# A two-layer attention trunk on one core: y loaded by 256 tokens, the last gate by token halves, score spans as steps of their own, and a running minimum

## The chip, the core and the metric

The kernel runs on one core of one Trainium2 chip. The metric is device time in microseconds of one execution; the kernel before has a median of 1973.18 us over 3 runs (1972.05 to 1976.23). The core has five engines that each work off their own queue in order: PE (TensorE; loads of weights are listed apart as PEld), DVE (VectorE), ACT (ScalarE), POOL (GpSimd) and SP (SyncE), which here issues every DMA.

## What is computed

The input x is 1024 tokens by 1024 channels in fp32. Two layers, each `h = h + rmsnorm(mixer(rmsnorm(h)))`; each mixer's input projection also gives a gate of the width of its output:

```python
for i in range(2):
    u = rmsnorm(h, norm_pre[i])
    y = dilated_mixer(u, ...) if i == 0 else diff_mixer(u, ...)
    h = h + rmsnorm(y, norm_post[i])
# diff_mixer, per head (8 heads, two parts c = 0, 1 of 64 channels, values of 128):
s = einsum(q, k) * scale                  # causal mask
p = softmax(s)
a = p[:, 0] - lam * p[:, 1]
o = rmsnorm(a @ v, subln) * (1 - lambda_init)
y = (o * silu(gate)) @ w_out
```

Layer 0 (dilated_mixer) has 16 heads in three groups of windows and dilations, whose outputs are weighed by their softmax denominators, then multiplied by silu(gate) and by the output weights in the same way.

## The kernel before

**Numbers and tiles.** PE multiplies fp32 values as a high and a low part, three matmuls for each product (hi by hi, hi by lo, lo by hi). `XH` and `XL` hold the two parts of the normalised input, transposed: 128 partitions, 8 blocks of channels (k-tiles), 1024 tokens. At the end of each layer the same two tiles are filled again with y, the gated output of the attention, for the product with the output weights.

**Stages of the span.** Up to about 400 us: values and gates of layer 0. To about 1210 us: the attention of layer 0 (scores L603, transposes L626, products L653 and L665). To about 1424 us: the output product of layer 0 (po L391), then values and most gates of layer 1. To about 1910 us: the attention of layer 1 (class DiffHead). The rest is the output product of layer 1.

**Filler.** In both attentions PE's order is written by hand: steps of the heads (a load, a block of scores, transposes, products, a norm, a gate) are sorted by a due time in units of heads, and after each step the class Filler issues matmuls of other work up to a goal that grows with the due time. That other work is, in this order: the projections of later heads' queries and keys (`qk_unit`, pqk L276; each is written to DRAM, `qk_d`, and read back by `heads_in`, L268 to L270), values, the last gates (`late_gates`, `gate_units`, pg L276), and `out_early` (L425), which forms the first half of the output product (pe L444) for 6 of the 8 token blocks from the first four k-tiles of y. Only PE's order is fixed by hand. The order of the other queues comes from a scheduler that builds on the program.

**The last gate and y.** y of the k-tiles 0 to 6 is written to DRAM (`put_y`, y_d L384) as its heads are done. The last gate is the last reader of the old XH and XL. It goes by k-tiles over both token halves, so that both PSUM banks of the tag `pj` are taken from its start: k-tiles 0 and 1 for half 0, then for half 1, then one k-tile at a time. `out_early` then loads y k-tile by k-tile (`load_y`, L402), each as two DMAs of 128 partitions x 1024 tokens, 512 KB, that follow the last reader of that k-tile. It yields until `stored` says that the k-tile's y is in DRAM. `part` (L449) is the copy of a block's partial output product out of PSUM; it is kept in XH and XL (L452), where the rows of the first k-tiles are free again, and read by the second part of the output product (`out_rest`, po L391).

**Heads of layer 1.** A DiffHead has two parts, s = 0 and 1. `load(part)` fetches queries (qh, ql) and keys (ka) of one part; both parts are due at h - 0.15, and the first also fetches the two value tiles vt, ahead of its queries and keys. The tiles qh, ql and ka have two buffers, so a head's two parts fill them and the next head's part can be loaded only when the last scores of the same part are done. `scores(i, s)` takes query block i: (i+1)*128 keys, in two spans of at most 512 columns from i = 4 on. Each span has two matmuls into a PSUM tile `sc` (tag `s`, 2 buffers), and a DVE instruction (L954, in the profile CUSTOM_DVE_ANT_0 with a read of its accumulator) that adds the mask, writes `pm` and gives the span's minimum. With two spans, L957 takes the smaller of both minima; for s = 0, L960 subtracts 10 ln 2 from it. ACT then takes the exponential (L961) with the sum as denominator `den`. For s = 1 DVE inverts it (L970), forms the factor k (L971) and combines both parts (L973). `transposes` (tp L984) splits the transposed result into ph (ACT, L989) and pl (DVE, L122), `product` multiplies by the values (ob L1004), `norm` and `gate` (L1045 to L1050) finish a half of 512 tokens and write y.

Of the kernel before, what the change touches and what calls it, by code (L numbers as in the profile page):

```python
# [10 lines left out]
F32 = mybir.dt.float32  # L11
# [20 lines left out]
SQ_LIMIT = 2.0 ** 64  # L32

# [3 lines left out]
SPAN, LAG, LAG_O, LAG_N, LAG_G, AHEAD = 0.85, 0.3, 0.2, 0.1, 0.15, 0.15  # L37
# [55 lines left out]
def trunk(ctx: ExitStack, tc: tile.TileContext, a: dict, out: bass.AP):  # L93
# [179 lines left out]
    def project(o, wh, wl, tok, kts=range(KT)):  # L273
        for kt in kts:
# [128 lines left out]

    def partial(n):
# [504 lines left out]
    with tc.tile_pool(name="l1", bufs=2) as lp:  # L909
        md = lp.tile([P, 640], F32, tag="md", name="md", bufs=1)  # L910
        nc.sync.dma_start(md, a["maskd"])
        class DiffHead:
# [7 lines left out]
            def load(self, part):  # L920
                fill.until(24 + self.h)
                fill.until(("v", self.h // 2))
                if part == 0:
                    self.den = lp.tile([P, NB], F32, tag="den", name="den")
                    self.fin = []
                    self.vt = []
# [6 lines left out]
                self.fin.append(heads_in(ep, 24 + self.h, part))  # L933

            def scores(self, i, s):
# [3 lines left out]
                if s == 0:  # L939
                    pm = lp.tile([P, wq], F32, tag=f"pm0{i}", name="pm0", bufs=1)  # L940
                else:
                    pm = lp.tile([P, T], F32, tag="pm1", name="pm1", bufs=1)
                mx = lp.tile([P, 4], F32, tag=f"mx{s}", name=f"mx{s}")
                den = self.den[:, i : i + 1] if s == 0 else mx[:, 3:4]
                cut = wq - max(256, wq - 512) if wq > 512 else 0
                spans = [(0, cut), (cut, wq)] if cut else [(0, wq)]
                for j, (k0, k1) in enumerate(spans):
                    w_ = k1 - k0
                    sc = ps.tile([P, 512], F32, tag="s", name="sc")
                    for k, q in enumerate((qh, ql)):  # L950
                        nc.tensor.matmul(  # L951
# [181 lines left out]
```

## Time and profile before

| | |
|---|---|
| median of 3 runs | 1973.18 us (1972.05 to 1976.23) |
| the profiled execution's own time | 1973.98 us |
| its span, first to last instruction | 1972.1 us |
| mean granted clock of PE | 0.986 |
| instructions | 29075 |
| ACT busy | 885.3 us (45%) |
| POOL busy | 784.2 us (40%) |
| bytes moved by DMA | 397.90 MB, 202 GB/s over the span |

The profile is of one execution. Its busy time by engine, the idle time ahead of an instruction with what ended it ("releaser"), tables of busy time by stretch of the span, and the granted clock of PE by stretch are read below. Times inside the span count from its start. 1973.98 - 1972.1 = 1.9 us of the execution lie outside the span.

### The profile page before, as it was taken

What the parts mean: (1) busy time and instruction counts of PE and PEld (TensorE: products, weight loads), DVE (VectorE), ACT (ScalarE), POOL (GpSimd) and SP (SyncE); (2) the same over time, 40 slices, a digit from 0 to 9 for tenths busy, and PEclk for the clock granted to TensorE, in tenths of its full rate; (3) what the DMA queues carried; (4) which work ended last, traced back from release to release, by engine and by line L of the source; (5) the groups of instructions that cost most, each with busy time, mean ns of one, the idle gap of its engine ahead of it and who ended that gap; (6) DMA issues with size and microseconds to landing.
All of it is one profiled execution on the core that took longest, in us unless ns stands there. A gap on an engine that the chain in (4) does not pass through costs nothing.

```text
span 1972.1 us, 29075 instructions
## 1 busy us (share of the span) xinstructions
PE 1888.0 (96%) x10008; PEld 1587.9 (81%) x10008; DVE 985.4 (50%) x2618; ACT 885.3 (45%) x2043; POOL 784.2 (40%) x553
## 2 busy tenths in 40 slices
PE   7999999999999999999999878999989899999897
PEld 5788888888888888888888767788878798897786
DVE  5311221135555555555555635550177877778626
ACT  4212112135656565656565555342244455446532
POOL 0000001154585867676776532320742435423011
PEclk9999999999999999999999979999999999999899
DMA  6424344277798989898989798442644565556643
GB/s 225 161 91 133 117 145 155 91 233 219 213 294 239 296 242 283 249 280 259 271 267 267 237 329 217 165 167 87 207 155 132 181 213 182 166 182 196 239 158 128
DMA packets 217539, 397.90 MB, mean 202 GB/s; under 512 B 40880, under 2 KB 123312, under 8 KB 217392
## 3 DMA queue, kind: packets, MB, share of 16 engines
q1 hardware_dynamic: 217392, 396.04, 63.8%
q8 instruction: 80, 1.31, 0.3%
q14 instruction: 67, 0.55, 0.1%
HBM read 254.87 MB, written 132.71 MB: 197 GB/s over the span
## 4 chain that ended last, share of the span: by engine, by line
PE 74%; DMA 10%; DVE 7%; POOL 3%; ACT 3%; issue 2%; SPq 1%; POOLq 0%; ACTq 0%; DVEq 0%
PE pqk L276 29%; PE pv L213 17%; PE pg L276 8%; PE po L391 4%; PE sc L603 3%; PE sc L951 3%; PE pe L444 2%; PE tp L626 2%; PE up L653 2%; PE ob L1004 2%; DMA ql<-qk_d 2%; DMA raw<-in_dil_w_out_dram 1%; DMA qk_d<-r 1%; PE tp L984 1%; DMA wb<-wt_d 1%
## 5 line engine op out<-in xcount | busy, mean ns | idle before, releaser
L276 PE MATMUL pqk<-XL,wh 128*128 128x512 f32 x1024 | 418.7, 409 | 0.0
L276 PE MATMUL pqk<-XH,wh 128*128 128x512 f32 x1024 | 408.3, 399 | 1.7 <-DVE t L252 1.7
L276 PE MATMUL pqk<-XH,wl 128*128 128x512 f32 x1024 | 408.6, 399 | 0.0
L122 POOL TENSOR_TENSOR wl<-raw,wh 128x1024 fp32r<-128x1024 f32 x59 | 141.7, 2401 | 512.3 <-ACT wh L184 509.7
L613 ACT ACTIVATE pm<-pm,st 128x128 f32<-128x128 f32 (+1 forms) x384 | 170.4, 444 | 149.5 <-DVE st L610 148.6
L276 PEld LDWEIGHTS pqk<-XH,wh 128*128 128x128 f32 x1024 | 193.2, 189 | 31.5 <-DVE t L252 3.5
L276 PEld LDWEIGHTS pqk<-XH,wl 128*128 128x128 f32 x1024 | 193.5, 189 | 26.9
L276 PEld LDWEIGHTS pqk<-XL,wh 128*128 128x128 f32 x1024 | 193.1, 189 | 26.9
L122 DVE TENSOR_TENSOR pp<-tp,pp 128x512 fp32r<-128x512 f32 (+2 forms) x192 | 104.3, 543 | 132.5 <-ACT pp L630 131.7
L184 ACT CAST wh<-raw 128x1024 fp32r<-128x1024 f32 x96 | 100.6, 1047 | 144.4 <-PE pqk L276 65.8
L961 ACT ACTIVATE pm<-pm,mx 128x256 f32<-128x256 f32 (+7 forms) x128 | 99.4, 777 | 126.8 <-DVE mx L960 61.1
L213 PE MATMUL pv<-vwh,XH 128*128 128x512 f32 x384 | 153.0, 398 | 2.0 <-ACT XH L158 2.0
L213 PE MATMUL pv<-vwh,XL 128*128 128x512 f32 x384 | 153.0, 398 | 2.0 <-DVE XL L122 1.3
L213 PE MATMUL pv<-vwl,XH 128*128 128x512 f32 x384 | 152.2, 396 | 0.0
L122 DVE TENSOR_TENSOR vs<-pv,vs 128x512 fp32r<-128x512 f32 x64 | 44.2, 690 | 202.2 <-ACT vs L518 194.7
L610 DVE CUSTOM_DVE_ANT_0 pm<-sc,masks 128x128 f32<-128x128 f32 (+1 forms) x384 | 119.1, 345 | 27.2 <-PE sc L603 26.5
L630 ACT CAST pp<-tp 128x512 fp32r<-128x512 f32 (+2 forms) x192 | 89.6, 467 | 80.7 <-PE up L653 62.2
L954 DVE CUSTOM_DVE_ANT_0 pm<-sc,md 128x512 f32<-128x512 f32 (+3 forms) x192 | 102.6, 551 | 38.0 <-PE sc L951 35.5
L122 DVE TENSOR_TENSOR wl<-raw,wh 128x1024 fp32r<-128x1024 f32 x37 | 49.1, 1326 | 137.0 <-ACT wh L184 136.7
L251 POOL TENSOR_TENSOR r<-t 128x512 f32<-128x512 f32 x64 | 84.4, 1319 | 80.2 <-DVE t L250 79.1
L518 ACT CAST vs<-pv 128x512 fp32r<-128x512 f32 x48 | 28.1, 586 | 186.8 <-PE pv L213 186.8
L276 PE MATMUL pg<-XH,wh 128*128 128x512 f32 x256 | 103.1, 403 | 5.0 <-DVE t L252 5.0
(514 smaller groups left out, 4435.4 us busy)
## 6 DMA issues: line engine op xcount, KB each, us to landing
qk_d<-rh SPq DMA_DIRECT2D x64, 512.0 KB
qk_d<-r SPq DMA_DIRECT2D x64, 512.0 KB
qh<-qk_d SPq DMA_DIRECT2D x128, 256.0 KB
ql<-qk_d SPq DMA_DIRECT2D x128, 256.0 KB
ka<-qk_d SPq DMA_DIRECT2D x64, 512.0 KB
v_d<-vs SPq DMA_DIRECT2D x48, 512.0 KB
raw<-in_dil_qk_dram SPq DMA_DIRECT2D x48, 512.0 KB
vt<-v_d SPq DMA_DIRECT2D x48, 512.0 KB
```

What stands on the lines that cost most here:

```text
L122: return eng.tensor_tensor(o, full, hi.bitcast(F32), ALU.subtract)
L184: nc.scalar.copy(wh, raw)
L213: nc.tensor.matmul(o, lhsT=l, rhs=r_, start=first and k == 0, stop=last and k == 3 * KT - 1, skip_group_check=True)
L251: nc.gpsimd.tensor_sub(put(r[0]), nat(t1), nat(t2))
L276: nc.tensor.matmul(o, lhsT=l[:, kt, :], rhs=r_[:, kt, tok], start=kt == 0 and k == 0, stop=kt == KT - 1 and k == 2)
L391: nc.tensor.matmul(banks[c], lhsT=l[:, kt, ts(n)], rhs=r_[:, ts(c, 512)], start=first and k == 0, stop=last and k == 2,)
L603: nc.tensor.matmul(sc[:, cols], lhsT=q[:, ts(b)], rhs=kv, start=k == 0, stop=k == 1)
L610: nc.vector.tensor_tensor_reduce(pm[:, cols], sc[:, cols], m[:, m.shape[1] - w_ :], 1.0, 3.0e38, ALU.add, ALU.min, st[:, 0, j : j + 1])
L613: nc.scalar.activation(pm[:, cols], pm[:, cols], AF.Exp, bias=st[:, 0, j : j + 1], scale=-1.0, accum_out=st[:, 1, j : j + 1])
L630: nc.scalar.copy(pp[:, 0, :w_], tp[:, :w_])
L954: nc.vector.tensor_tensor_reduce(pm[:, k0:k1], sc[:, :w_], m_, 1.0, 3.0e38, ALU.add, ALU.min, mx[:, j : j + 1])
L961: nc.scalar.activation(pm[:, :wq], pm[:, :wq], AF.Exp, bias=mx[:, 0:1], scale=-1.0, accum_out=den)
```

## The change

Four edits, in both layers where both have the code.

1. The last gate goes by token halves like every other gate: all 8 k-tiles of tokens 0 to 511 in one bank, then all of tokens 512 to 1023 in another. After each half, `load_early` issues y of the first four k-tiles for that half's tokens: four DMAs of 128 partitions x 4 k-tiles x 256 tokens (512 KB each, in rows of 1 KB where a k-tile's row was 4 KB). `out_early` no longer loads them, nor waits for `stored`.
2. In layer 1 a head's queries and keys are loaded ahead of its values; part 0 is due at h - 1 + 0.85 * (56 + 0.76 * 8) / 72 = h - 0.267, part 1 at h - 0.173, and the values come with part 1.
3. A score span is a step of its own, `scores(i, s, j)`, due at (s + (j + 0.5)/n) of the block, so that filler can come between two spans of a block.
4. The second span's DVE instruction starts from the first span's minimum instead of 3.0e38, so that L957 is gone. The shift by 10 ln 2 (L960) is gone too: ph and pl are scaled by 2^-10 instead (ACT's CAST becomes an ACTIVATE with a scale, DVE's subtraction a SCALAR_TENSOR_TENSOR), and two constants of the norm carry the factor.

```diff
+DEN_SHIFT = 2.0 ** -10
-SPAN, LAG, LAG_O, LAG_N, LAG_G, AHEAD = 0.85, 0.3, 0.2, 0.1, 0.15, 0.15
+SPAN, LAG, LAG_O, LAG_N, LAG_G = 0.85, 0.3, 0.2, 0.1, 0.15
...
             if prepare and f == fs[-1]:
                 prepare()
-                banks = [ps.tile([P, 512], F32, tag="pj", name="pg") for _ in range(2)]
-                for kts in ((0, 1), *((kt,) for kt in range(2, KT))):
-                    for c in range(2):
-                        yield from project(banks[c], wh, wl, ts(c, 512), kts)
-                for c in range(2):
-                    yield f, c, banks[c]
-                return
             for c in range(2):
                 o = ps.tile([P, 512], F32, tag="pj", name="pg")
                 yield from project(o, wh, wl, ts(c, 512))
+                if prepare and f == fs[-1]:
+                    load_early(layer, c)
                 yield f, c, o
...
+    def load_early(layer, c):
+
+        for b in (2 * c, 2 * c + 1):
+            for e, x in enumerate((XH, XL)):
+                nc.sync.dma_start(
+                    x[:, :EARLY, ts(b, 256)].bitcast(F32),
+                    y_d[layer][:EARLY, e, :, ts(b, 256)].rearrange("k p t -> p k t"))
...
         ws[EARLY - 1] = out_weights(pool, w, EARLY - 1)
-        for kt in range(EARLY):
-            while (layer, kt) not in stored:
-                yield None
-            load_y(layer, kt)
...
+                self.fin.append(heads_in(ep, 24 + self.h, part))
+                if part:
                     self.vt = []
...
-                self.fin.append(heads_in(ep, 24 + self.h, part))
-
+            @staticmethod
+            def spans(i):
+
+                wq = (i + 1) * P
+                cut = wq - max(256, wq - 512) if wq > 512 else 0
+                return [(0, cut), (cut, wq)] if cut else [(0, wq)]
...
-            def scores(self, i, s):
+            def scores(self, i, s, j):
...
+                k0, k1 = self.spans(i)[j]
+                w_ = k1 - k0
...
-                    nc.vector.tensor_tensor_reduce(
-                        pm[:, k0:k1], sc[:, :w_], m_, 1.0, 3.0e38, ALU.add, ALU.min, mx[:, j : j + 1])
-                if cut:
-                    nc.vector.tensor_tensor(mx[:, 0:1], mx[:, 0:1], mx[:, 1:2], ALU.min)
-                if s == 0:
-
-                    nc.vector.tensor_scalar_add(mx[:, 0:1], mx[:, 0:1], -10 * math.log(2.0))
+                nc.vector.tensor_tensor_reduce(
+                    pm[:, k0:k1], sc[:, :w_], m_, 1.0, mx[:, 0:1] if j else 3.0e38,
+                    ALU.add, ALU.min, mx[:, j : j + 1])
+                if k1 < wq:
+                    return
                 nc.scalar.activation(
-                    pm[:, :wq], pm[:, :wq], AF.Exp, bias=mx[:, 0:1], scale=-1.0, accum_out=den)
+                    pm[:, :wq], pm[:, :wq], AF.Exp, bias=mx[:, j : j + 1], scale=-1.0, accum_out=den)
...
-                nc.scalar.copy(ph[:, :w_], tp[:, :w_])
-                low(nc.vector, pl[:, :w_], tp[:, :w_], ph[:, :w_])
+                nc.scalar.mul(ph[:, :w_], tp[:, :w_], DEN_SHIFT)
+                nc.vector.scalar_tensor_tensor(
+                    pl[:, :w_], tp[:, :w_], DEN_SHIFT, ph[:, :w_].bitcast(F32), ALU.mult, ALU.subtract)
...
-                nc.vector.scalar_tensor_tensor(d2, d2, SQ_LIMIT, sm[:, 0:4], ALU.mult, ALU.is_gt)
+                nc.vector.scalar_tensor_tensor(d2, d2, SQ_LIMIT * DEN_SHIFT ** 2, sm[:, 0:4], ALU.mult, ALU.is_gt)
...
-                steps.append((h - AHEAD, lambda hd=hd, part=part: hd.load(part)))
+                due = h - 1 + SPAN * (NB * (NB - 1) + (part + 0.76) * NB) / 72
+                steps.append((due, lambda hd=hd, part=part: hd.load(part)))
...
+                n = len(hd.spans(i))
                 for s in range(2):
-                    due = h + SPAN * (i * (i + 1) + (s + 0.5) * (i + 1)) / 72
-                    steps.append((due, lambda hd=hd, i=i, s=s: hd.scores(i, s)))
+                    for j in range(n):
+                        due = h + SPAN * (i * (i + 1) + (s + (j + 0.5) / n) * (i + 1)) / 72
+                        steps.append((due, lambda hd=hd, i=i, s=s, j=j: hd.scores(i, s, j)))
```

How instructions move, at three places. First the queue of SP at the end of layer 0, up to the keys `ka` of the second to last head. qh, ql and ka are loads of queries and keys, raw is a block of output weights, sil_in the gate, XH and XL from y_d are y. Before:

```order
L421 DMA raw<-in_dil_w_out_dram 128x1024
L402 DMA XL<-y_d_63 128x1024
L753 DMA wb<-wt_d 64x512 x2
L763 DMA sil_in<-sil_d_65 128x512
L699 DMA st_d<-sr 8x128 x3
L384 DMA y_d_63<-u 128x512
L699 DMA st_d<-sr 8x128
L268 DMA qh<-qk_d 64x1024 x2
L322 DMA sil_d_65<-sil 128x1024
L384 DMA y_d_63<-u 128x512
L268 DMA ql<-qk_d 64x1024 x2
L270 DMA ka<-qk_d 128x1024
```

After:

```order
L398 DMA XL<-y_d_63 128x1024
L699 DMA st_d<-sr 8x128 x4
L269 DMA qh<-qk_d 64x1024 x2
L318 DMA sil_d_65<-sil 128x1024
L753 DMA wb<-wt_d 64x512 x2
L269 DMA ql<-qk_d 64x1024
L380 DMA y_d_63<-u 128x512
L269 DMA ql<-qk_d 64x1024
L271 DMA ka<-qk_d 128x1024
L763 DMA sil_in<-sil_d_65 128x512
L702 DMA st_d<-st 128x2x4 x2
L425 DMA raw<-in_dil_w_out_dram 128x1024 x2
```

Ahead of this `ka` stand twelve loads of y of 512 KB each before and ten after, eight of them in the new shape. The raw load and the sil_in load stood ahead of it and stand behind it.

Second the queue of SP at the end of layer 1, around the keys of head 7. The last `ka` of each piece is that of part 1; y_d from sq and os is half of the y of head 6 on its way to DRAM. Before:

```order
L322 DMA sil_d_66<-sil 128x1024
L402 DMA XL<-y_d_64 128x1024
L402 DMA XH<-y_d_64 128x1024
L421 DMA raw<-in_diff_w_out_dram 128x1024
L268 DMA qh<-qk_d 64x1024 x2
L268 DMA ql<-qk_d 64x1024 x2
L384 DMA y_d_64<-sq 128x512
L384 DMA y_d_64<-os__17548 128x512
L270 DMA ka<-qk_d 128x1024
L1049 DMA sil_in<-sil_d_66 128x512
```

After:

```order
L271 DMA ka<-qk_d 128x1024
L404 DMA XH<-y_d_64 128x4x256
L404 DMA XL<-y_d_64 128x4x256
L404 DMA XH<-y_d_64 128x4x256
L380 DMA y_d_64<-sq 128x512
L380 DMA y_d_64<-os__17444 128x512
L269 DMA qh<-qk_d 64x1024 x2
L269 DMA ql<-qk_d 64x1024 x2
L271 DMA ka<-qk_d 128x1024
L404 DMA XL<-y_d_64 128x4x256
```

Before, one k-tile of y (XL and XH) stands ahead of the queries and keys of part 1. After, three of the four loads of half 0 stand there. The stores of y stood between ql and ka, and stand ahead of qh.

Third the queue of DVE in layer 1, at the block of 768 columns of head 6. ISA is the instruction of a score span and the read of its minimum; pm1 and mx1 belong to part 1, pm0 and mx0 to part 0; RECIPROCAL and the two instructions with neg_lam and pm0 on both sides finish a block. Before:

```order
L973 SCALAR_TENSOR_TENSOR pm0_17470<-pm1_17486,mx1_17487,pm0_17470 128x640
L1018 TENSOR_SCALAR sq_17549<-os__17548 128x512
L954 ISA pm1_17565,mx1_17566<-sc_17567,md_13031 128x512
L954 ISA mx1_17566 128x1
L954 ISA pm1_17565,mx1_17566<-sc_17571,md_13031 128x256
L954 ISA mx1_17566 128x1
L122 TENSOR_TENSOR pl_17558<-tp_17556,ph_17557 128x512
L957 TENSOR_TENSOR mx1_17566<-mx1_17566 128x1
L970 RECIPROCAL mx1_17566<-mx1_17566 128x1
L971 SCALAR_TENSOR_TENSOR mx1_17566<-mx1_17566,neg_lam_12648,den_17210 128x1
L122 TENSOR_TENSOR pl_17585<-tp_17583,ph_17584 128x384
L973 SCALAR_TENSOR_TENSOR pm0_17521<-pm1_17565,mx1_17566,pm0_17521 128x768
```

After:

```order
L979 SCALAR_TENSOR_TENSOR pm0_17370<-pm1_17386,mx1_17387,pm0_17370 128x640
L962 ISA pm1_17460,mx1_17461<-sc_17462,md_13031 128x512
L962 ISA mx1_17461 128x1
L997 SCALAR_TENSOR_TENSOR pl_17453<-tp_17451,ph_17452 128x512
L962 ISA pm1_17460,mx1_17461<-sc_17468,md_13031,mx1_17461 128x256
L962 ISA mx1_17461 128x1
L962 ISA pm0_17479,mx0_17480<-sc_17481,md_13031 128x512
L962 ISA mx0_17480 128x1
L976 RECIPROCAL mx1_17461<-mx1_17461 128x1
L977 SCALAR_TENSOR_TENSOR mx1_17461<-mx1_17461,neg_lam_12648,den_17047 128x1
L979 SCALAR_TENSOR_TENSOR pm0_17419<-pm1_17460,mx1_17461,pm0_17419 128x768
```

Before, the two spans of a block stand next to each other or one instruction apart, and the inversion that waits for ACT's exponential follows them directly. After, the first span of the next block (sc_17481) stands between the second span and the inversion. Over all 64 blocks with two spans, before has at most one instruction between the two spans' pairs in 60, and after in 20.

More of the change, by code (lines that the diff above doesn't have):

```diff
@@ L271, in heads_in, with project @@
         return qh, ql, ka
-    def project(o, wh, wl, tok, kts=range(KT)):
-        for kt in kts:
+    def project(o, wh, wl, tok):
+        for kt in range(KT):
             for k, (l, r_) in enumerate(((wh, XH), (wh, XL), (wl, XH))):
@@ new lines, in scores @@
+                if j == 0:
+                    pm = (lp.tile([P, wq], F32, tag=f"pm0{i}", name="pm0", bufs=1) if s == 0
+                          else lp.tile([P, T], F32, tag="pm1", name="pm1", bufs=1))
+                    self.now = pm, lp.tile([P, 4], F32, tag=f"mx{s}", name=f"mx{s}")
+                pm, mx = self.now
+                den = self.den[:, i : i + 1] if s == 0 else mx[:, 3:4]
+                k0, k1 = self.spans(i)[j]
+                w_ = k1 - k0
+                sc = ps.tile([P, 512], F32, tag="s", name="sc")
@@ new lines, in scores @@
+                for k, q in enumerate((qh, ql)):
+                    nc.tensor.matmul(
+                        sc[:, :w_], lhsT=q[:, ts(i)], rhs=ka[:, k0:k1], start=k == 0, stop=k == 1)
+                m_ = md[:, 640 - w_ :] if k1 == wq else md[:, :w_]
+                nc.vector.tensor_tensor_reduce(
[3 more added lines that the diff above has]
+                    return
```

16 lines of the change are left out of this document (1 added, 15 removed).

## The prediction

> **What bounds the kernel now.** The page first: busy time by engine.
>
> ```profile
> PE 1888.0 (96%) x10008; PEld 1587.9 (81%) x10008; DVE 985.4 (50%) x2618; ACT 885.3 (45%) x2043; POOL 784.2 (40%) x553
> ```
>
> PE is the bound: 1888.0 of 1972.1 us. The change leaves every matmul in place, so it can only win from the 84 us in which PE stands still, and from time at a lower clock. Next, the table of busy time by stretches, at the end of layer 0 and in layer 1:
>
> ```profile
> 1120.00:1160.00 40.00, 30.94 (x140) 25.29 (x141) 15.37 (x43) 20.43 (x48) 20.46 (x14) 0.76 1.05 352
> 1160.00:1200.00 40.00, 34.89 (x198) 29.88 (x197) 16.31 (x56) 22.15 (x63) 8.16 (x6) 0.91 1.02 299
> 1440.00:1480.00 40.00, 35.52 (x227) 32.10 (x226) 30.76 (x79) 19.77 (x38) 15.01 (x10) 0.96 0.44 141
> 1640.00:1680.00 40.00, 36.53 (x204) 30.45 (x203) 33.11 (x81) 20.69 (x42) 22.64 (x15) 1.00 0.66 211
> ```
>
> The columns after the length are PE, PEld, DVE, ACT, POOL, PE's granted clock, the DMA share and GB/s. From 1120 to 1200 PE loses 14 of 80 us, and the DMA engines are full (1.05, 1.02). In layer 1 they are not (0.44, 0.66), while DVE works 31 to 33 of 40 us. What PE waits for, 1095 to 1300 us:
>
> ```profile
> PE pe L444 <- DMA XH<-y_d: 6.1, 3, 4.4
> PE sc L603 <- DMA st_d<-st: 5.1, 1, 5.1
> PE po L391 <- ACT part L449: 3.1, 1, 3.1
> ```
>
> A fourth wait there is in the page's row of the gates' matmuls (mean 403 ns, 5.0 us idle ahead of them):
>
> ```profile
> L276 PE MATMUL pg<-XH,wh 128*128 128x512 f32 x256 | 103.1, 403 | 5.0 <-DVE t L252 5.0
> ```
>
> And over the whole span, of layer 1:
>
> ```profile
> PE sc L951 <- DVE mx L954: 17.9, 16, 2.5
> PE sc L951 <- DMA ka<-qk_d: 7.8, 2, 6.7
> ```
>
> These six are 45 of the 84 us. After a long stall PE also runs at half clock, as the pieces behind two of them show:
>
> ```profile
> 1120.00:1125.00 5.00, 4.39 (x14) 3.86 (x15) 3.40 (x4) 2.03 (x3) 4.36 (x3) 0.50 1.11 248
> 1150.00:1155.00 5.00, 4.34 (x13) 3.08 (x13) 0.00 (x0) 1.87 (x6) 0.00 (x0) 0.51 1.06 390
> 1155.00:1160.00 5.00, 3.52 (x13) 2.71 (x12) 1.20 (x5) 1.20 (x6) 0.00 (x0) 0.50 1.03 420
> 1120.61 0.79 PE L276 MATMUL pg<-XH,wh 128*128 128x512 f32 x1 [4.97 <-DVE t L252]
> 1150.40 0.80 PE L444 MATMUL pe<-wh,XH 128*128 128x512 f32 x1 [4.38 <-DMA XH<-y_d]
> ```
>
> Busy time times the missing clock is 2.2 + 2.1 + 1.8 = 6.1 us.
>
> **The change part by part.** *The last gate by halves and y by 256 tokens, layer 0.* The 5.0 us at 1120.61 are the second `pj` bank, held by rotary products of the last query/key unit. By halves, it is asked for 24 matmuls later (24 x 403 ns = 9.7 us), so this wait goes. The 6.1 us for y go if all k-tiles of 256 tokens arrive while the second half's 24 matmuls run. Were PE the only limit, that gives 5.0 + 6.1 + 6.1 = 17.2 us. It isn't: DMA is full, and the next wait is behind it.
>
> ```profile
> 1170.69 0.58 SPq L270 DMA_DIRECT2D ka<-qk_d  x1
> 1176.27 0.45 PE L603 MATMUL sc<-ka,qh 128*128 128x128 f32 x1 [5.11 <-DMA st_d<-st]
> ```
>
> The row names st_d, but the matmul reads `ka`, issued 5.6 us earlier behind all the y loads. PE reaching this point sooner only waits longer. What brings `ka` sooner is what no longer stands ahead of it on SP: two y loads, a raw load (0.5 MB each) and a sil_in (0.25 MB), 1.84 million bytes, at the stretch's 352 GB/s 5.2 us. Against that stand rows of 1 KB instead of 4 KB. No row of before shows such loads alone; the nearest full stretches carry 248 (with other small packets) and 420 GB/s. Eight loads are 4.19 million bytes: 16.9 or 10.0 us, so between 0 and +6.9 us. I take a quarter, 1.7, since the 248 also holds stores and rows shorter than 1 KB. Net 5.2 - 1.7 = 3.5 us, ends -1.7 (a loss) and 17.2.
>
> The Trainium skill, DMA: Bandwidth & Descriptors, section Specifications, gives 512 B as the smallest transfer at line rate. By it the smaller rows would cost nothing and this term be 5.2 us; no run so far shows 1 KB rows by themselves.
>
> *The `part` copy.* `po` waits 3.1 us at 1231.90 for a copy that ACT takes up only behind its casts of y (the first of two is shown):
>
> ```profile
> 1228.34 0.62 ACT L374 CAST XH<-u 128x512 fp32r<-128x512 f32 x1 [2.46 <-DVE u L764]
> 1231.28 0.57 ACT L449 COPY part<-pe 128x512 f32<-128x512 f32 x1
> 1231.90 1.19 PE L391 MATMUL po<-ow,XH 128*128 128x512 f32 x2 [3.14 <-ACT part L449]
> 1230.00:1235.00 5.00, 3.10 (x7) 2.47 (x8) 2.90 (x3) 1.85 (x3) 0.00 (x0) 0.70 0.51 137
> ```
>
> In the changed queue it stands ahead of them, and that removes the 3.1 us and 0.9 of half clock (3.10 x 0.30). But DVE now puts three weight splits ahead of `XL<-u`, which PE needs a dozen us later. Between 0 and 4.0 I take half, 2.0. Layer 0 gives 5.5 us.
>
> *Spans apart and the minimum (layer 1).* The removed and the altered instructions, the inversion that waits for ACT, and L1047 as the nearest row to the new form of pl:
>
> ```profile
> L957 DVE TENSOR_TENSOR mx<-mx 128x1 f32<-128x1 f32 x64 | 22.8, 357 | 0.7
> L960 DVE TENSOR_SCALAR mx<-mx 128x1 f32<-128x1 f32 x64 | 9.5, 148 | 0.7
> L970 DVE RECIPROCAL mx<-mx 128x1 f32<-128x1 f32 x64 | 10.3, 161 | 31.5 <-ACT pm L961 31.3
> L122 DVE TENSOR_TENSOR pl<-tp,ph 128x512 fp32r<-128x512 f32 x48 | 32.8, 684 | 1.9 <-ACT ph L989 1.9
> L1047 DVE SCALAR_TENSOR_TENSOR os__15635<-os__15635,subln,rt 128x512 f32<-128x512 f32 x1 | 0.7, 748 | 0.0
> ```
>
> DVE loses 22.8 + 9.5 = 32.3 us; the 80 pl instructions (48 of this size, 32 smaller) in the form of L1047 cost at most 80 x 64 ns = 5 us more. Net 27 us over 64 two-span blocks and 64 shifts. What that is worth shows at the longest stall:
>
> ```profile
> 1454.63 2.39 POOL L122 TENSOR_TENSOR wl<-raw,wh 128x1024 fp32r<-128x1024 f32 x1 [3.95 <-ACT wh L184]
> 1455.27 1.76 DVE L957 TENSOR_TENSOR mx<-mx 128x1 f32<-128x1 f32 x1
> 1457.13 0.94 ACT L961 ACTIVATE pm<-pm,mx 128x768 f32<-128x768 f32 x1 [2.09 <-DVE mx L957]
> 1458.19 0.16 DVE L970 RECIPROCAL mx<-mx 128x1 f32<-128x1 f32 x1 [1.16 <-ACT pm L961]
> 1459.68 1.99 DVE L973 SCALAR_TENSOR_TENSOR pm<-pm,mx,pm 128x768 f32<-128x768 f32 x1
> 1461.59 0.68 DVE L954 CUSTOM_DVE_ANT_0 pm<-sc,md 128x512 f32<-128x512 f32 x1
> 1462.33 0.50 PE L951 MATMUL sc<-ka,qh 128*128 128x512 f32 x1 [2.53 <-DVE mx L954]
> ```
>
> PE wants a score bank back; its reader L954 stands on DVE behind minimum (1.76), wait for the exponential (1.16) and combination. After, the minimum is gone, the exponential starts that much sooner, and the wait for it lies behind the next block's first span in the queue instead of ahead of it. Against a full gain: a bank is still two spans from its next use, and L973's 1.99 us stay. So of 16 stalls with a mean of 1.1 us each loses the mean minimum, 0.36, and half of the mean wait for the exponential, 31.3 / 64 / 2 = 0.25: 10 of the 17.9 us. The ends are 3 (27 / 128 = 0.21 us for each stall) and 17 (nearly all). To this comes the half clock after the stalls, 0.04 x 35.52 = 1.4 us in 1440 to 1480: 11.4 in all.
>
> L957 starts under POOL's `wl` and ends with it (1454.63 + 2.39 = 1457.02 and 1455.27 + 1.76 = 1457.03). The Trainium skill, SBUF — State Buffer, section Who interferes with whom, has the mechanism: a DVE instruction with two SBUF inputs and a GpSimd one that reads SBUF exclude each other, and the later one blocks until the first is done. The two ends agree with it; rival 3 is what it does here.
>
> *Head 7's keys.* 6.7 us at 1833.42, with 1.6 x 0.5 + 5.0 x 0.45 = 3.0 us of half clock after it:
>
> ```profile
> 1833.42 0.47 PE L951 MATMUL sc<-ka,qh 128*128 128x128 f32 x1 [6.75 <-DMA ka<-qk_d]
> 1830.00:1835.00 5.00, 1.58 (x6) 1.48 (x7) 0.30 (x2) 0.46 (x2) 0.00 (x0) 0.50 1.04 413
> 1835.00:1840.00 5.00, 5.00 (x23) 4.50 (x22) 2.82 (x9) 1.22 (x4) 0.23 (x1) 0.55 1.03 411
> ```
>
> The earlier due time buys a fiftieth of a head for part 1 (0.023 x 60 = 1.4 us), but SP is in order: part 1 now stands behind three y loads that wait for the gate's half 0, where it had two, and behind two stores of y. 0.5 MB more at 413 GB/s is 1.3 us. That cancels: 0, ends -9 (a gain) and +5. Part 0, 7 us sooner, removes at most 1.1 of the 7.8; the values, later, are wanted only 0.3 + 0.2 of a head into it.
>
> *At nothing:* ACT's scaling in ph (ACT works some 20 of 40 us), the norm constants, and the dropped yields for `stored`: they hold matmuls back only in the written order, and the loads still follow the stores on SP.
>
> Sum: 1973.98 - 5.5 - 11.4 = 1957.1 for the profiled execution, 0.8 above the median, so 1956.3.
>
> **The rivals.**
> 1. *Only PE limits the end of layer 0.* For: DMA's share also counts loads wanted much later, and 1.84 MB of them move away. Against: 1.05 and 1.02. Then 17.2 + 4.0 + 11.4 = 32.6: 1940.6.
> 2. *DMA takes layer 0's gain back.* For: the queue is full from 1120 on, the same bytes have to pass before the last heads' keys and before `po` can go on, and 1 KB rows at 248 GB/s cost 6.9 where the shorter queue gave 5.2. Against: 390 and 420 GB/s in 1150 to 1160, where most of the packets are y's. Only layer 1 gains: 1973.2 - 11.4 = 1961.8.
> 3. *L957's stalls are passed on.* What it waited for POOL, the next DVE instruction with two SBUF inputs (L971 or L973) waits in its place. For: the 1.76 us that end with POOL's `wl`. Against: the exponential starts ahead of that wait all the same. DVE is relieved of 64 short instructions at about L960's 148 ns instead of 22.8 us: 9.5 + 9.5 - 5 = 14 us, half of 27, so layer 1 gives 5.7: 1962.0.
> 4. *The banks' distance decides, not DVE's work.* With two `s` banks a matmul waits for the reader of the span before last; spaced evenly or in pairs, that is one block earlier. For: the longest stall still has L973 and an L954 ahead of the freed bank, 2.7 us. Against: the 27 us are 7% of DVE's work there (32 of each 40 us over the 480 us of that stage). Layer 1's waits stay, layer 0 gives 5.5: 1967.7.
> 5. *Nothing moves:* 2 and 4 together, 1973.2; also the case that the freed time is taken by waits that stand right behind those removed.
> 6. *Slower: DVE stands before the second span.* DVE is in order; the second span now comes at least two 0.4 us matmuls later, and where DVE has nothing else queued ahead of it, up to 64 x 0.8 = 51 us of standing still come to a queue that saves 27. DVE has 6.9 us to spare in 1640 to 1680. If PE's waits on L954 then double, 17.9 and 1.4 come on top, less 5.5: 1987.0. It decides from the point where these waits grow by 5.5 us, a third. For it: L970 already idles 1.16 us for the exponential in that way. Against it: in most blocks other work stands between the spans in the new queue, so that DVE has something to do.
>
> **How the numbers follow.** Chances: forecast 0.36, rival 1 0.10, 2 0.16, 3 0.08, 4 0.08, 5 0.10, 6 0.12. About 0.2% or 4 us can be told from no change here. Faster by more: 0.36 + 0.10 + 0.16 + 0.08 + 0.08 less 0.04 for the weak end of 4, 0.74; within 0.2%: 0.10 + 0.03, 0.13; slower 0.12 + 0.01, 0.13. The range leaves out rival 6 and half of rival 1: from 1940, about 1's number, to 1975, 5's with 2 of the 5 us by which head 7 may lose.
>
> **What would show it.** Right: no wait of pg for L252 and none of pe for y near 1120 to 1160, the DMA share still above 1 there; `sc` L603 still waiting for keys, but 3 to 4 us sooner in the span; the sum of sc's waits on mx near 8 us; the ka stall of head 7 of 5 to 10 us. Wrong: y's loads at well under 350 GB/s with PE waiting on them; DVE idle ahead of the second spans with PE's waits at 18 us or more; a stall of head 7 above 15 us.

## The result and the profile after

The changed kernel takes 1996.01 us (median of 4 runs, 1994.62 to 1998.11) against 1974.51 us of the kernel before (4 runs beside them, 1972.05 to 1976.23): a ratio of 1.0112, 95% interval 1.0096 to 1.0128. It is slower by 22 us where 17 us of gain were forecast, and lies outside the range. The profiled execution took 1994.62 us with a span of 1992.8 us; the mean granted clock is 0.981 (0.986 before).

What PE waits for over the whole span, the largest of the changed stages (us in total, times, longest):

```profile
PE sc L958 <- DMA ka<-qk_d: 32.8, 7, 10.0
PE sc L603 <- DMA ka<-qk_d: 10.2, 2, 8.2
PE sc L958 <- DVE mx L962: 9.4, 12, 1.5
PE tp L990 <- DVE pm L979: 7.3, 6, 2.2
PE sc L603 <- issue: 5.7, 1, 5.7
PE pe L444 <- ACT part L449: 2.6, 1, 2.6
```

The waits for a score bank fell from 17.9 to 9.4 us. But the waits of the layer 1 scores for keys grew from 7.8 us in 2 places to 32.8 in 7: one for every head from the second on. At the end of layer 0 the waits for y and for the `pj` bank are gone, and keys are waited for instead. Three of the same stretches as before, and one in which the keys are late:

```profile
1120.00:1160.00 40.00, 28.65 (x154) 23.98 (x154) 16.66 (x53) 23.30 (x57) 18.77 (x14) 0.83 1.08 337
1160.00:1200.00 40.00, 29.44 (x156) 23.75 (x154) 14.09 (x48) 20.68 (x59) 8.79 (x7) 0.90 1.01 310
1440.00:1480.00 40.00, 37.91 (x274) 34.95 (x274) 29.71 (x71) 21.18 (x38) 12.66 (x8) 1.00 0.56 172
1600.00:1640.00 40.00, 32.98 (x216) 30.49 (x215) 23.55 (x67) 17.48 (x38) 6.28 (x4) 0.91 0.53 167
```

The last of these in the kernel before, and, in the changed kernel, the 7 us of it in which PE waits for keys:

```profile
1600.00:1640.00 40.00, 38.29 (x262) 35.08 (x262) 30.32 (x92) 19.46 (x42) 8.20 (x6) 1.00 0.53 176
1601.00:1608.00 7.00, 0.00 (x0) 0.00 (x0) 0.15 (x1) 0.00 (x0) 0.00 (x0) 0.76 1.05 302
```

The DMA engines are as full at the end of layer 0 as they were (1.08, 1.01). In layer 1 their mean share over 40 us is about a half, but that mean hides a burst: in the wait itself they are full (1.05). The five loads that PE waits for are 1.5 MB (four of 256 KB and one of 512), by estimate 5.2 us at these 302 GB/s, and other transfers run among them. The clock is below 1 where it was 1.00 before: in 1600 to 1640 it is 0.91, and 0.09 x 33 busy us are another 3 us. In 1440 to 1480 it rose from 0.96 to 1.00, as the prediction had it.

Where the time went by stages shows in the first and the last score of layer 1 and, between them, in one reload of keys. Four rows of PE's timeline of the kernel before:

```profile
1431.88 0.22 PE L951 MATMUL sc<-ka,qh 128*128 128x128 f32 x1
1591.66 0.39 PE L951 MATMUL sc<-ka,ql 128*128 128x512 f32 x1
1606.13 0.33 PE L951 MATMUL sc<-ka,qh 128*128 128x128 f32 x1 [1.06 <-DMA ka<-qk_d]
1872.85 0.39 PE L951 MATMUL sc<-ka,qh 128*128 128x512 f32 x1
```

And the same four of the changed kernel:

```profile
1427.68 0.22 PE L958 MATMUL sc<-ka,qh 128*128 128x128 f32 x1
1591.20 0.39 PE L958 MATMUL sc<-ka,ql 128*128 128x512 f32 x1
1608.00 0.47 PE L958 MATMUL sc<-ka,qh 128*128 128x128 f32 x1 [7.02 <-DMA ka<-qk_d]
1893.07 0.39 PE L958 MATMUL sc<-ka,qh 128*128 128x512 f32 x1
```

Layer 1 begins 4.2 us sooner (1431.88 to 1427.68); how much of that the change gave is taken up below, under layer 0. From its first to its last score it takes 465.4 us instead of 441.0: 24.4 us lost. The waits for keys alone are 25.0 us more; the rest, 8.5 us gained at the banks against 4.7 more of the transposes' waits and the lower clock, about cancels.

The two rows in the middle are the loop that matters. A part's queries and keys have two buffers, one for each part. The last score of part 1 of a head (1591.59 at its end) frees them, SP issues five loads, and the next head's first score of part 1 needs them. The row before and after with the time from the one to the other as its stretch:

```profile
1592.05:1606.13 14.08, 11.97 (x100) 11.33 (x98) 9.26 (x24) 5.87 (x13) 2.22 (x2) 1.00 1.03 358
1591.59:1608.00 16.41, 8.37 (x70) 7.92 (x68) 7.38 (x18) 4.33 (x9) 1.19 (x2) 0.90 1.04 328
```

After, PE has work until 1608.00 - 7.02 = 1600.98, that is 9.4 us; the loop takes 16.4. Before, the last score ends at 1592.05 and PE has work until 1605.07, 13.0 us, in a loop of 14.1. The DMA engines were full in this loop before the change too (1.03 and 1.04). SP's part of it, in the changed kernel (start, time to issue):

```profile
1594.92 0.45 SPq L269 DMA_DIRECT2D qh<-qk_d  x1
1595.47 1.36 SPq L858 DMA_DIRECT2D v_d<-vs  x2
1597.83 0.45 SPq L269 DMA_DIRECT2D qh<-qk_d  x1
1598.50 1.72 SPq L269 DMA_DIRECT2D ql<-qk_d  x2
1600.45 0.39 SPq L271 DMA_DIRECT2D ka<-qk_d  x1
```

The last of the five, `ka`, is issued 8.9 us after the last score, and the keys are there 7.5 us after that. So this loop needs about 16 us, and the matmuls between must cover it. All seven loops of part 1, from the same timelines (us; the head is the one that waits, and work is PE's time from the last score to the wait or, where there is none, to the score):

| head | work before | work after | `ka` issued after the last score, before | the same, after | loop after | wait before | wait after |
|---|---|---|---|---|---|---|---|
| 1 | 12.1 | 8.8 | 2.2 | 3.8 | 12.3 | 0 | 3.6 |
| 2 | 12.6 | 9.7 | 5.3 | 4.0 | 11.2 | 0 | 1.5 |
| 3 | 13.0 | 9.4 | 7.0 | 8.9 | 16.4 | 1.1 | 7.0 |
| 4 | 11.3 | 8.4 | 4.9 | 3.3 | 10.1 | 0 | 1.7 |
| 5 | 11.6 | 8.8 | 2.4 | 7.5 | 15.1 | 0 | 6.4 |
| 6 | 11.1 | 7.8 | 3.5 | 2.7 | 10.5 | 0 | 2.7 |
| 7 | 9.3 | 7.5 | 7.3 | 8.9 | 17.5 | 6.7 | 10.0 |

PE's work between shrank at every head, from 81.0 to 60.4 us in all. The loop is not the same at every head: where SP issues `ka` only 7.5 to 8.9 us after the last score, at the heads 3, 5 and 7, stand 23.4 of the 32.8 us. No score of part 0 waits for keys in either kernel.

### The profile page after: what moved, and what is told of

Read it like the earlier page. It is cut to its first block, busy times and chain, and to the rows that moved or that the text cites. A ratio compares the mean times of both kernels' runs of the same rounds, so it can differ in the third digit from the quotient of the medians.

```text
span 1992.8 us, 29013 instructions
## 1 busy us (share of the span) xinstructions
PE 1890.4 (95%) x10008; PEld 1592.4 (80%) x10008; DVE 972.2 (49%) x2490; ACT 890.0 (45%) x2043; POOL 782.4 (39%) x553
## 4 chain that ended last, share of the span: by engine, by line
PE 78%; DMA 9%; DVE 6%; ACT 2%; issue 2%; POOL 2%; SPq 1%; POOLq 0%; DVEq 0%; ACTq 0%
PE pqk L277 31%; PE pv L214 17%; PE pg L277 8%; PE sc L603 4%; PE po L387 3%; PE tp L626 3%; DMA ka<-qk_d 3%; PE sc L958 3%; PE up L653 3%; PE pe L444 2%; PE ob L1012 2%; PE tp L990 1%; DMA XL<-y_d 1%; DVE pm L962 1%; DMA st_d<-st 1%
## 5 line engine op out<-in xcount | busy, mean ns | idle before, releaser
L958 PE MATMUL sc<-ka,qh 128*128 128x512 f32 (+2 forms) x192 | 73.2, 381 | 42.3 <-DMA ka<-qk_d 32.8
L603 PE MATMUL sc<-ka,qh 128*128 128x128 f32 (+1 forms) x384 | 95.2, 272 | 16.9 <-DMA ka<-qk_d 10.2
```

Source lines behind the costliest of these rows:

```text
L603: nc.tensor.matmul(sc[:, cols], lhsT=q[:, ts(b)], rhs=kv, start=k == 0, stop=k == 1)
L958: nc.tensor.matmul(sc[:, :w_], lhsT=q[:, ts(i)], rhs=ka[:, k0:k1], start=k == 0, stop=k == 1)
```

## The experiments

The theory is called cover: edit 3 puts the last score span of a head later in PE's order, so that fewer matmuls stand between it and the next head's first score. Counted in PE's order at 0.40 us per 512 columns, part 1 has 17 us of them before and 11.4 after (head 7: 12.5 and 8.2), part 0 has 22.6 and 15.9. That count compares orders and is not a time: in the trace of the kernel before, matmuls of 256 columns start 0.12 us apart at full clock (1592.01, 1592.13, 1592.25), and the table above has 11 to 13 us where the count has 17. The first rival, called queue, is that edit 2's earlier loads block SP; the second is that separate spans cost by themselves, on DVE. Ratios are to the kernel before on the same chip.

**Edit 3 undone, the other three kept.**

```diff
-                    for j in range(n):
-                        due = h + SPAN * (i * (i + 1) + (s + (j + 0.5) / n) * (i + 1)) / 72
-                        steps.append((due, lambda hd=hd, i=i, s=s, j=j: hd.scores(i, s, j)))
+                    due = h + SPAN * (i * (i + 1) + (s + 0.5) * (i + 1)) / 72
+                    steps.append((due, lambda hd=hd, i=i, s=s, n=n: [hd.scores(i, s, j) for j in range(n)]))
```

> The changed kernel with edit 3 undone: both spans of a block in one step, due as before; the other three edits stay. Theory (cover): a head's keys, queries can be reloaded only after the last scores of the same part, and the change moved these scores later in PE's order, so that between them and the first scores of the next head stand 11.4 instead of 17.1 us of matmuls for part 1 (columns by 0.40 us per 512) and 15.9 instead of 22.6 for part 0. Undone, the waits for ka fall from 32.8 to under 10 us, and the time to about 1965 us: 1974.5 less 4.2 at the end of layer 0 and some 5 of the waits on DVE. Rival (queue): the earlier, reordered loads of edit 2 block SP; then the waits for ka stay near 30 us and the time near 1995.

1968.01 us, ratio 0.9972 (0.9957 to 0.9986).

```profile
PE sc L958 <- DVE mx L962: 18.0, 21, 2.3
PE sc L958 <- DMA ka<-qk_d: 6.8, 3, 3.9
```

The waits for keys are down to 6.8 us, with edit 2 in place: the queue is not it. But the waits for a score bank are back at 18.0 us, although the minimum is gone; the expected 5 us of gain on DVE did not come.

**Edit 3 alone on the kernel before.** The scores as in the changed kernel, with the minimum (L957) and the shift (L960) kept behind the second span:

```diff
+                if k1 < wq:
+                    return
+                if j:
+                    nc.vector.tensor_tensor(mx[:, 0:1], mx[:, 0:1], mx[:, 1:2], ALU.min)
```

> The kernel before with edit 3 alone: each span a step of its own, with the separate minimum, the shift, the loads and the gate of before. Cover: waits for ka near 33 us as in the changed kernel, time 1993 to 2002. Queue: the loads are those of before, so waits for ka near 8 us and a time at or under 1974.

1998.15 us, ratio 1.0117 (1.009 to 1.0143).

```profile
PE sc L957 <- DMA ka<-qk_d: 23.7, 6, 7.9
PE tp L993 <- DVE pm L982: 16.4, 7, 6.7
PE sc L957 <- DVE mx L961: 8.7, 12, 1.8
```

Edit 3 alone makes a loss as large as that of all four. The keys have a smaller part of it than expected, and a second wait has most of the rest: the transposes of the last query blocks, whose due times are fixed, come to wait for `pm`, since the last scores are later. SP issues `ka` late at the heads 3, 5 and 7 here too (8.7, 7.2 and 7.8 us after the last score), with the loads of before. And the waits for a bank fall to 8.7 us with the minimum still there.

**The last block's spans together, the rest separate.** In the changed kernel block 7 alone gets the step of the first experiment.

```diff
+                    if i == NB - 1:
+                        due = h + SPAN * (i * (i + 1) + (s + 0.5) * (i + 1)) / 72
+                        steps.append((due, lambda hd=hd, i=i, s=s, n=n: [hd.scores(i, s, j) for j in range(n)]))
+                        continue
```

> The changed kernel, but the spans of the last query block alone (i = 7) are in one step again, due as before; blocks 4 to 6 keep separate spans. The cover is 16.9 and 21.8 us again. Cover: waits for ka under 10 us, waits on DVE near the 9 us of the changed kernel or a little more, time 1960 to 1968. If the separate spans themselves cost, by DVE standing before the second span, three quarters of it stay: 1985 or more.

1964.56 us, ratio 0.9942 (0.9925 to 0.996).

```profile
PE sc L958 <- DVE mx L962: 12.7, 16, 2.2
PE sc L958 <- DMA ka<-qk_d: 6.8, 3, 3.4
```

Three of four separate blocks cost nothing that shows; the loss comes from where the last one stands. This is faster than both kernels.

**Edit 1 alone on the kernel before:** `project`, `gate_units`, `load_early` and `out_early` as in the change's diff.

> The kernel before with edit 1 alone: the last gate by halves, y by 256 tokens, in both layers. Layer 0's end 4 us sooner as in the changed kernel. Cover: in layer 1 only head 7's keys can change, between 0 and +5 us, so 1970 to 1975. If y by 256 tokens in rows of 1 KB disturbs the last head's keys, their wait grows from 6.7 to 10 us or more and the 4 us are given back: 1975 to 1980.

1971.76 us, ratio 0.9982 (0.9966 to 0.9998).

```profile
PE sc L602 <- DMA ka<-qk_d: 12.2, 2, 7.5
PE sc L950 <- DMA ka<-qk_d: 4.2, 2, 3.5
```

The first score of layer 1 starts 0.2 us later than before in this execution, but the execution was 1.8 us behind already at 1036 us, ahead of everything that the edit alters; the section on the prediction compares all runs from there. The waits for y became waits for keys in the full DMA queue. In layer 1 head 7's keys wait 3.5 instead of 6.7 us; with edit 4 alone, which doesn't touch them, it was 4.0, so one execution doesn't show that this is edit 1's doing.

**One number changed in the kernel before:**

```diff
-SPAN, LAG, LAG_O, LAG_N, LAG_G, AHEAD = 0.85, 0.3, 0.2, 0.1, 0.15, 0.15
+SPAN, LAG, LAG_O, LAG_N, LAG_G, AHEAD = 0.89, 0.3, 0.2, 0.1, 0.15, 0.15
```

> The kernel before with one number changed: SPAN 0.89 instead of 0.85, so that the scores of a head spread over more of it and the last ones come later. Pairs of spans, minimum, shift, loads and gate are those of before. The matmuls between the last scores of a part and the next head's first come to 11.4 and 15.9 us, as in the changed kernel. Cover: waits for ka 20 to 33 us, time 1990 to 2000. If the loss needed separate spans (bank order, DVE's queue) or the new loads, nothing of it shows here: 1970 to 1978.

2006.13 us, ratio 1.0166 (1.0121 to 1.0212).

```profile
PE tp L984 <- DVE pm L973: 15.8, 6, 3.3
PE sc L951 <- DMA ka<-qk_d: 15.6, 4, 6.8
```

Nothing of the change is in this kernel but the lateness of a head's last scores, and it loses at least as much as the change did. The time came out above the expected 1990 to 2000, and the split was missed: keys 15.6 us, and as much again of the transposes waiting for `pm`. Where PE already waits for `pm`, the keys have that time to come: with edit 3 alone, head 2 waits 6.7 us for `pm` in its loop and not at all for keys. So lateness has two prices, and the theory named one.

**All four edits, the scores of a head earlier:** SPAN 0.78 in the changed kernel.

```diff
-SPAN, LAG, LAG_O, LAG_N, LAG_G = 0.85, 0.3, 0.2, 0.1, 0.15
+SPAN, LAG, LAG_O, LAG_N, LAG_G = 0.78, 0.3, 0.2, 0.1, 0.15
```

> The changed kernel, all four edits, with SPAN 0.78 instead of 0.85: all spans separate, but the last ones as early as before; cover 16.9 and 22.4 us. Cover: waits for ka under 10 us, waits of the transposes for pm under 3 us, waits for a score bank between 9 and 18 us since the scores stand closer, time 1958 to 1968. If separate spans cost something by themselves: over 1980.

1964.95 us, ratio 0.9951 (0.9934 to 0.9969).

```profile
PE sc L958 <- DVE mx L962: 14.5, 15, 2.2
PE sc L958 <- DMA ka<-qk_d: 1.7, 2, 1.0
```

One number turns the loss of 1.1% into a gain of 0.5%, every span separate.

**All four edits, block 7's spans a quarter of a block earlier.**

```diff
-                        due = h + SPAN * (i * (i + 1) + (s + (j + 0.5) / n) * (i + 1)) / 72
+                        due = h + SPAN * (i * (i + 1) + (s + (j + 0.5) / n - (0.25 if i == 7 and n == 2 else 0)) * (i + 1)) / 72
```

> The changed kernel with the spans of block 7 a quarter of a block earlier, still separate (j = 0 at s, j = 1 at s + 0.5): cover 16.5 and 20.6 us. Cover: waits for ka near 7 us, waits for a score bank 9 to 13 us, time 1960 to 1967, like the run with the last block paired. If separate spans of the last block cost by themselves: 1975 or more.

1964.4 us, ratio 0.9948 (0.9925 to 0.9972); waits for a bank 12.4 us, for keys 8.3. As expected: it is the place of the last spans, not that they are separate. SP issues `ka` of head 5 here 2.2 us after the last score instead of 7.5, so the late issue goes with the late score too; what it meets on SP was not tested.

**Edit 2 undone in the changed kernel:** load order and due times of before.

```diff
+                steps.append((h - AHEAD, lambda hd=hd, part=part: hd.load(part)))
-                due = h - 1 + SPAN * (NB * (NB - 1) + (part + 0.76) * NB) / 72
-                steps.append((due, lambda hd=hd, part=part: hd.load(part)))
```

> The changed kernel with edit 2 undone: both parts' loads due at h - 0.15, values ahead of keys. The cover stays 11.4 and 15.9 us. Cover: still slow, 1993 to 2000 us, waits for ka 24 to 33 us. Queue: back at 1965 to 1975, waits for ka under 10 us.

2000.04 us, ratio 1.0127 (1.0108 to 1.0146).

```profile
PE sc L957 <- DMA ka<-qk_d: 31.6, 7, 8.9
```

The queue falls a second time: with the loads of before the keys are as late.

**Edit 4 alone on the kernel before:** the chained minimum and the scaling of ph and pl, with pairs of spans.

```diff
-                        pm[:, k0:k1], sc[:, :w_], m_, 1.0, 3.0e38, ALU.add, ALU.min, mx[:, j : j + 1])
+                        pm[:, k0:k1], sc[:, :w_], m_, 1.0, mx[:, 0:1] if j else 3.0e38,
+                        ALU.add, ALU.min, mx[:, j : j + 1])
-                if cut:
-                    nc.vector.tensor_tensor(mx[:, 0:1], mx[:, 0:1], mx[:, 1:2], ALU.min)
```

> The kernel before with edit 4 alone: the second span starts from the first one's minimum, L957 and L960 gone, the shift in ph and pl; spans in pairs, loads and gate of before. Cover unchanged, 16.9 and 22.6 us, so waits for ka near 8 us. If the forecast's size for the minimum was right, the waits for a score bank fall from 17.9 to about 8 us by this edit and the time to 1963 to 1967. If the spacing of the spans and not the minimum shortened them, they stay at 15 to 18 us and the time at 1970 to 1976.

1973.85 us, ratio 0.9998 (0.9984 to 1.0011). PE's waits, then DVE's inversion:

```profile
PE sc L952 <- DVE mx L955: 17.1, 19, 2.3
```

```profile
L967 DVE RECIPROCAL mx<-mx 128x1 f32<-128x1 f32 x64 | 10.4, 162 | 33.7 <-ACT pm L958 33.7
```

No difference can be told, and 17.1 of 17.9 us of waits stay. The edit takes 32 us of work off DVE, less 4 us that the chained form costs (last section), and nothing of it shows at PE: the inversion still waits for the exponential, 33.7 us in all, 31.3 before.

**Edit 2 alone on the kernel before:** `load` and its due times as in the change's diff.

> The kernel before with edit 2 alone: keys ahead of values, part 0 due at h - 0.267, part 1 at h - 0.173. Cover as before. Both theories of the loss put it elsewhere by now: 1970 to 1976, waits for ka 4 to 10 us. A loss of over 10 us would bring the rival of the queue back as a second cause.

1974.88 us, ratio 1.0006 (0.9994 to 1.0017), waits for keys 8.9 us. Nothing, as expected.

**All four edits with still more cover:** SPAN 0.74.

```diff
-SPAN, LAG, LAG_O, LAG_N, LAG_G = 0.85, 0.3, 0.2, 0.1, 0.15
+SPAN, LAG, LAG_O, LAG_N, LAG_G = 0.74, 0.3, 0.2, 0.1, 0.15
```

> The changed kernel with SPAN 0.74: cover 22.6 us for both parts and 17.0 for head 7's part 1 (12.5 at 0.78). Cover: what is left of the waits for ka goes, head 7's among them, under 3 us in all; the scores stand closer, so waits for a score bank 15 to 22 us. Time 1958 to 1968. If 17 us of cover are already enough everywhere, it is no faster than with 0.78.

1972.55 us, ratio 0.9997 (0.9984 to 1.0009).

```profile
PE sc L958 <- DVE mx L962: 20.0, 23, 3.3
PE sc L958 <- DMA ka<-qk_d: 1.4, 1, 1.4
```

The waits for keys are gone as expected, but so is the gain: the scores stand so close that the waits for a bank pass those of the kernel before. From the first score of layer 1 to the end of the span this execution takes 539.4 us, the one at 0.78 takes 532.9, and the 5.5 us more at the banks are most of that. Another 3 us between the two executions lie ahead of layer 1, where SPAN sets no step; their cause is open.

**Edits 1 and 3 only, block 7 earlier:** the kernel of edit 3 alone, with edit 1's code and the due time of the run with block 7 earlier.

> The kernel before with edit 1 and edit 3 only, the spans of block 7 a quarter of a block earlier so that the cover stays 16.5 and 20.6 us; the separate minimum, the shift and the loads of before stay. If edits 2 and 4 are worth nothing, as they were alone, this is as fast as the four edits with the same cover: 1962 to 1968 us, waits for a score bank 9 to 13 us, for ka near 8. If the minimum pays once the spans stand apart, it is 4 us or more slower than that: 1968 to 1974.

1969.74 us, ratio 0.9988 (0.9971 to 1.0004).

```profile
PE sc L956 <- DVE mx L960: 11.0, 13, 1.8
PE sc L956 <- DMA ka<-qk_d: 9.2, 4, 3.5
```

The time speaks for edits 2 and 4 being worth 5 us by the medians, or 8 by the ratios (0.9988 against 0.9948, on two chips), once the spans are apart. But the waits are near those of the run with all four (12.4 and 8.3), and the intervals touch (0.9971 and 0.9972). That stays open.

## Why the prediction was wrong

**The step that failed is "Head 7's keys".** It weighed the reload of keys for head 7 alone, and by the order of SP alone ("That cancels: 0, ends -9 and +5"). The order of PE was not in it, nor were the other six heads. For head 7 the wait grew by 3.3 us, within the ends that were given; for the heads 1 to 6, put at nothing, it grew from 1.1 to 22.8 us. Edit 3 moves each head's last span, and with it the moment from which the buffers are free. The due time moves by 0.85 x 0.25 x 8 / 72 = 0.024 of a head, 1.4 us, as much as the loads' due time was said to buy; but filler owed since the step ahead of a step is issued behind it, so that the two spans, set apart, left less behind the last one. In the row pair above, PE's work fell from 13.0 to 9.4 us. With loops of 10 to 17.5 us the loss came at every head: 25.0 us, of which 20.6 are work that no longer stands between; the rest is that the loops are longer (table above).

The prediction had the row for it, ka 7.8 us in 2 places, and read the small number as room. It also took the smaller of the two, 1.06 us at 1606.13, for a wait of part 0, which edit 2 was to remove; it is head 3's part 1, the loop shown above. The experiments with SPAN, the two with block 7 and edit 3 undone show that the late last scores are the cause; that the same lateness makes the transposes wait is shown by the experiments with edit 3 alone and SPAN 0.89, up to 16 us. What the prediction named as signs of being right came about for the most part (no wait of pg and pe, DMA share 1.08, waits for a bank at 9.4 us, head 7's stall 10.0 us): none of them looked at the heads 1 to 6.

**"Spans apart and the minimum": size near, reason more than half wrong, and in part luck.** Forecast 10 of 17.9 us, measured 8.5. But 0.36 of the 0.61 us for each stall were put on the minimum, and the minimum by itself gave 0.8 us. The spacing gave it: 8.7 us were left with the minimum kept. And where the spans are apart and the keys come sooner, more is left than in the changed kernel: 12.4 us with block 7 earlier, 11.0 with edits 1 and 3. So the spacing is worth 5.5 to 6.9 us there; that the rest of the 8.5 came while PE stood waiting for keys is likely, but not shown. Rows of DVE from 1420 to 1900, one of the kernel before, five of the changed one, and one with edit 3 undone:

```profile
L954 DVE CUSTOM_DVE_ANT_0 pm<-sc,md 128x512 f32<-128x512 f32 (+3 forms) x192 | 102.6, 551 | 38.0 <-PE sc L951 35.5
L962 DVE CUSTOM_DVE_ANT_0 pm<-sc,md 128x512 f32<-128x512 f32 (+3 forms) x128 | 72.5, 570 | 60.5 <-PE sc L958 58.1 <-DVE pm L979 0.5
L962 DVE CUSTOM_DVE_ANT_0 pm<-sc,md,mx 128x256 f32<-128x256 f32 (+2 forms) x64 | 37.1, 580 | 20.4 <-PE sc L958 19.4
L976 DVE RECIPROCAL mx<-mx 128x1 f32<-128x1 f32 x64 | 10.3, 161 | 16.9 <-ACT pm L967 16.2
L979 DVE SCALAR_TENSOR_TENSOR pm<-pm,mx,pm 128x128 f32<-128x128 f32 (+3 forms) x64 | 62.4, 975 | 1.7
L977 DVE SCALAR_TENSOR_TENSOR mx<-mx,neg_lam,den 128x1 f32<-128x1 f32 x64 | 22.9, 357 | 1.8
L962 DVE CUSTOM_DVE_ANT_0 pm<-sc,md,mx 128x256 f32<-128x256 f32 (+2 forms) x64 | 37.0, 579 | 3.0
```

DVE now stands 58.1 + 19.4 = 77.5 us ahead of score spans, 35.5 before, and the inversion waits 16.2 instead of 31.3 us. Half of the 77.5 is not rival 6's: 38.6 us (13.9 before) stand ahead of spans of 128 columns, the first of each part, where PE itself waits for keys. But its own wait is there: ahead of the second spans stand 19.4 us, and 3.0 with edit 3 undone (last row). Its price, a doubling of PE's waits for a bank, is not: they halved. So rival 6 is right only in that the kernel is slower, by luck, since the loss came from the keys. Rival 4 was half right: DVE's work doesn't decide, the order does.

**Rival 3, stalls passed on,** is not seen: the two instructions that were to inherit them, L977 and L979, keep their means (357 and 975 ns; 387 and 980 before, in the rows of the same stretch). One other short DVE instruction, the square of the denominators (nd), grew from 302 to 553 ns, 4 us over its 16; with the minimum kept (edits 1 and 3) it has 465 ns, so most of that isn't the minimum's stall. The SBUF — State Buffer page of the Trainium skill, section Who interferes with whom, explains L957's own stall; no run here shows that stall going on to another instruction.

**Layer 0** was forecast to gain 5.5 us, of which 3.5 by the shorter queue. Of the 4.2 us above the change gave the smaller part. Up to 1110 us both kernels give PE, DVE, ACT, POOL and SP the same work in the same order, yet the 615th of the 768 score matmuls of layer 0 starts at 1032.2 us after and 1034.6 before: 2.4 of the 4.2 us are chance. From that matmul to the first score of layer 1 the five kernels without edit 1 take 397.3 to 401.5 us (median 397.9), the nine with it 393.1 to 396.5 (median 395.5). So edit 1 is worth some 2.4 us there; the run with edit 1 alone has 395.7.

As said, DMA is full and the keys are late there: the listed waits come to 6.1 + 5.1 + 5.0 + 3.1 = 19.3 us before, and 10.2 + 5.7 + 2.6 = 18.5 after. What else differs is the clock (0.76 to 0.83 in 1120 to 1160). The wait of `po` for the `part` copy did not go, as the term of 2.0 us had it, but shrank and moved: pe and po wait 1.75 + 3.14 us for it before and 2.64 + 1.40 after. The removed wait for the second bank was also worked out with 24 x 403 ns; 403 ns is how long one matmul is busy, but they overlap and start 0.23 us apart at full clock (1114.11, 1114.34, 1114.57 before), so 24 take 5.5 us. The wait went all the same. The upper end of 6.9 us for rows of 1 KB was too wide: in 1120 to 1160 of the changed kernel the trace has packets of 1024 bytes at a mean of 20.6 GB/s for one DMA engine, and packets of 4096 bytes at 20.7. The Trainium skill's 512 B for the smallest transfer at line rate (DMA: Bandwidth & Descriptors, Specifications) agrees with that.

**The pl instructions** cost nothing instead of 5 us; the chained span costs 4 us that the prediction didn't have (below). Neither mattered.

## What to carry to other kernels

A wait of nearly nothing is not room: where buffers are reused, work out the loop from the last reader through the issuing queue to the landing, and compare it with the work that stands between the two in the written order, at every turn of the loop and not only where the profile shows a wait. A step that is split or moved later carries the release of everything that it reads last; here that cost 25 us where the spacing itself gained 5 to 8, and moving the last piece back made a gain of the loss. A mean DMA share over a long stretch is no proof of free bandwidth: 0.53 over 40 us held a wait at 1.05. Freed time on an engine is worth little if what stands behind it waits for another one: 28 us less on DVE gave nothing by themselves.

## What the runs showed of the hardware

The span instruction that takes its start from a column in SBUF is slower by the same 60 ns at each width than the one that starts from a constant; the form is not in the profile of before. Rows of the changed kernel by form:

```profile
L962 DVE CUSTOM_DVE_ANT_0 pm<-sc,md 128x512 f32<-128x512 f32 x64 | 43.9, 686 | 9.6 <-PE sc L958 8.9
L962 DVE CUSTOM_DVE_ANT_0 pm<-sc,md,mx 128x512 f32<-128x512 f32 x16 | 11.9, 746 | 4.3 <-PE sc L958 4.2
L962 DVE CUSTOM_DVE_ANT_0 pm<-sc,md 128x384 f32<-128x384 f32 x32 | 17.7, 552 | 2.5 <-PE sc L958 1.0 <-DVE pm L979 0.5
L962 DVE CUSTOM_DVE_ANT_0 pm<-sc,md,mx 128x384 f32<-128x384 f32 x16 | 9.8, 614 | 7.1 <-PE sc L958 7.1
L997 DVE SCALAR_TENSOR_TENSOR pl<-tp,ph 128x512 fp32r<-128x512 f32 x45 | 30.8, 685 | 4.6 <-ACT ph L996 4.4
```

746 against 686 ns and 614 against 552 ns, and 480 against 420 ns at 256 columns: 64 times 60 ns are the 4 us. And a subtraction out of PSUM with a scale on its first input takes as long as one without (685 ns, 684 before), which the nearest row, 748 ns, had not shown: that row had other operands.
